# Up projection with half products from the second pair on, and residual loads in order of use

## The chip, the core and the metric

The kernel runs on one core of a Trainium2 chip. Its engines are TensorE (matmul; PE in the profile, with its weight loads as PEld), VectorE (DVE), ScalarE (ACT), GpSimd (POOL) and SyncE (SP), which issues most DMAs. The metric is the device time of one execution in microseconds.

## The reference

One layer of an encoder block on 512 tokens of width 1024, in float32: an input layernorm, a mixing part (a state-space scan beside an attention branch), a layernorm, a convolutional feed-forward network (FFN) of inner width 2816, and a last layernorm. The change lies in the FFN and at the two layernorms around it:

```python
def _conv_ffn(h, w_up, conv_w, conv_b, w_down):
    u = _causal_dwconv(h @ w_up, conv_w, conv_b)
    a, v = jnp.split(u, 2, axis=-1)
    return (jax.nn.silu(a) * v) @ w_down
...
        h = _layernorm(DN_ALPHA * h + mix.astype(h.dtype), ln1_g[l], ln1_b[l])
        f = _conv_ffn(h, ffn_w_up[l], ffn_conv_w[l], ffn_conv_b[l], ffn_w_down[l])
        h = _layernorm(DN_ALPHA * h + f.astype(h.dtype), ln2_g[l], ln2_b[l])
```

## The kernel before

**Arithmetic.** TensorE multiplies in a reduced form of float32 (fp32r). So that little is lost, each operand is split into a high part (ScalarE copies and rounds it) and a low part (VectorE takes the difference), and each product is three passes: high by high, low weight by high, high weight by low. A block of 128 output channels over all 1024 inputs and 512 tokens is 8 input tiles x 3 passes = 24 passes of 512 columns. A weight block is loaded by SP into one of four raw buffers (`wraw`), and split into one of three pairs `whi`, `wlo`.

**Up projection.** The 5632 outputs are 22 pairs: pair n holds 128 channels of the half `a` and the same 128 of the half `v`. `ORDER` lists the pairs in the order in which they are done. Pairs 0 to 3 are done as ordinary blocks. The first three blocks (pair 0 and half of pair 1) are done in two halves of the tokens, `slice(0, 256)` first, so that they can begin while the layernorm of the last token tiles still runs; the next five are whole. The 18 pairs in `SEVEN` go through `seven`: the pair of blocks is a 2x2 block matrix (two channel halves by two input halves of 512), the activation is one too (two input halves by two token halves, L_ and R_), and the product is made from seven half products rather than eight. Each half product is 4 input tiles x 3 passes = 12 passes of 256 columns.

Its seven half products need sums of blocks. The sums of the weights (`su_d` in DRAM) are formed ahead by DMA, in four steps a pair: a copy issued by SP (two transfers), and three adding DMAs issued by POOL (`add`), each of which waits for a split on VectorE (`last_lo`) so that they are spread. The list `ahead` holds these steps in order; `ahead_run(n)` runs the next n of them: every seventh step of the scan stage (`SUMS`, as long as more than 6 are left) and, for the last 6, in the up loop. The sums of the activation, T(0) to T(3) (`Thi`, `Tlo`), are formed by `form_T` from `h32`, a transposed copy of the layernorm's output: four sums or differences on VectorE, four high parts on ScalarE, four low parts on VectorE, each 128x1024. T(1) multiplies `y2`, T(2) `y3`, T(0) `y1` and T(3) `a22`; `a11`, `a12` and `y4` multiply plain activation. `chain[0]` makes TensorE's matmuls follow the program's order; elsewhere a list scheduler sets the order of an engine by priority and simulated time, with weight loads 400 places ahead (`high_priority`).

**Before it** stand the merge loop (`for n in range(KD)`, the attention branch's output blocks `w_br_att`), the output projection `w_out` and the layernorm. The layernorm goes by four token tiles of 128: statistics on VectorE, the root on POOL (`rs_y`), scaling on VectorE and POOL, transposes on TensorE into two PSUM buffers (`ptr`), and the eviction: high part and `h32` by ScalarE, low part (`h1lo`) by VectorE. The normalized tiles are also stored to `h1_d` as the residual for the end.

**After it** `up_out` adds the taps of the convolution (four operations on VectorE a pair) and the gate. The down projection is made of half products too; its VectorE and ScalarE operations are put in the order of written keys (`plan`, `at`), in microseconds from its start: `early` gives the keys of the weight blocks of its second part (17 of them, `w_next`), each split by `parts(k, k + 1.2, ...)`. The residual tiles are loaded again from `h1_d` during its first part, tiles 0 to 3 at c = 6 to 9; the additions (`res`) use tiles 2 and 3 first.

Of the kernel before, what the change touches and what calls it, by code (L numbers as in the profile page):

```python
# [16 lines left out]
P = 128  # L17
T = 512
# [56 lines left out]
def block_kernel(ctx, tc, A, out):  # L75
# [91 lines left out]
    last_pow, last_w, last_lo = [None], [None], [None]  # L167
# [9 lines left out]
    def split(hi, lo, src):  # L177
        nc.scalar.activation(hi, src, AF.Copy)  # L178
        return nc.vector.tensor_tensor(lo, src, hi.bitcast(F32), OP.subtract)  # L179
# [911 lines left out]
    ahead_run(len(ahead) - 6)  # L1091
# [78 lines left out]
    for n in range(KD):  # L1170
# [5 lines left out]
        proj(p, w, yT, part=(first, NP))  # L1176
        nc.vector.scalar_tensor_tensor(sg, sg, 1.0, p, OP.add, OP.mult)
# [26 lines left out]
    for k in range(KW, KD):  # L1204
        wo[k] = w_halves("w_out", k)
    l1r = {(n, j): wt("v", [P, T], "l1" + n) for j in range(2) for n in "gb"}
# [3 lines left out]
    for i in range(NT):  # L1210
# [8 lines left out]
        for j in range(2):  # L1219
# [12 lines left out]
            split(h1hi[:, ks, tok(i)], h1lo[:, ks, tok(i)], tr)  # L1232
            nc.scalar.activation(h32[j][:, :, tok(i)], tr, AF.Copy)
# [80 lines left out]

    def up_out(m, pa, pb):
# [6 lines left out]
        for j, p in enumerate((pa, pb)):  # L1322
# [3 lines left out]
            at(S, k(j, 0), nc.scalar.activation(y, p, AF.Identity, bias=fb[:, c:c + 1], scale=taps[2]))  # L1326
# [22 lines left out]
    def form_T():  # L1349

        b11, b12, b21, b22 = [t[:, :, c] for t in h32 for c in (L_, R_)]
        nc.vector.tensor_tensor(b11, b11, b12, OP.subtract)
        nc.vector.tensor_tensor(b12, b22, b12, OP.subtract)
        yield
        nc.vector.tensor_tensor(b22, b22, b11, OP.add)
        nc.vector.tensor_tensor(b21, b22, b21, OP.subtract)
        yield
        for j, t in ((1, b22), (2, b12), (0, b11), (3, b21)):
            if j == 1:
                nc.scalar.activation(Thi[:, j], t, AF.Copy, scale=-1.0)  # L1360
                nc.vector.scalar_tensor_tensor(Tlo[:, j], t, -1.0, Thi[:, j].bitcast(F32), OP.mult, OP.subtract)
            else:
                split(Thi[:, j], Tlo[:, j], t)
            if j == 2:
                yield
        yield
# [13 lines left out]
    def seven(m):  # L1380
# [18 lines left out]
        bank, W = tr_tile(), acc_tile()  # L1399
# [5 lines left out]
        product(W[:, R_], y3, Tq[2], first=True)  # L1405
        if m > 4:
            product(W[:, L_], a12, Bq[1, 0])
        product(U, y2, Tq[1])
        copy(2)
        if m == 4:  # L1410
            product(W[:, L_], a12, Bq[1, 0])
        yield
        y1, = w_block(S_[:, 1])
        product(U, y1, Tq[0])
# [31 lines left out]
    started = []  # L1446
    for s in range(3, 2 * KF + 1):
# [4 lines left out]
        if s < 8:  # L1452
            p = acc_tile() if s % 2 else any_tile("abc")
            proj(p, w_("w_up", 2 * ORDER[s // 2] + s % 2), h1T)
            pend.append(p)
        elif s == 2 * KF:
            pend += next(started.pop(0))
            chain[0] = False
        elif s % 2 == 0:
            if not started:  # L1460
                chain[0], last_pe[0] = True, None
            started.append(seven(s // 2))
# [4 lines left out]
        if s > 3:  # L1467
            with tc.issue_after(last_lo[0].ins):
                next(T_steps, None)
        if s == 36:  # L1470
            mark = last_w[0]
        if s >= 8 and s % 2 == 0:
# [3 lines left out]
        if s == 3:  # L1476
            for i in range(NT):
# [348 lines left out]
```

## Time and profile before

| | |
|---|---|
| median of 3 runs | 1072.49 us (1071.71 to 1072.97) |
| profiled execution, its own time | 1072.7 us |
| profiled execution, span of the trace | 1071.0 us |
| granted TensorE clock | 0.998 |
| DMA | 221.01 MB, mean 206 GB/s |

The page is read as follows. The busy line tells how long each engine ran; matmuls are pipelined, so a busy PE can still lose time by a slow pace, which is seen from the starts of its passes. The chain of waits follows the work that ended last back to the start, so pieces of one engine that follow each other without a gap are time that this engine alone sets. A row of a timeline gives start, length, engine, line, operation, output and inputs, and in brackets the idle time before it and what ended that. `L179` is a helper (`split`), so its operations are told apart by their tiles: `wlo` a weight block, `h1lo` the activation, `Tlo` a sum.

The stages that matter here, from the trace: merge loop and output projection from about 640 us, first pass of the up projection 728.5 us, first half product 775.4 us, down projection from 956.8 us, last matmul 1063.6 us, end 1071.0 us.

### The profile page before, as it was taken

The numbers are of one execution on the slowest core, as the hardware profiler recorded it, in microseconds if no ns is written. First come the engines' busy times: TensorE is split into PE (matmuls) and PEld (weight loads), VectorE is DVE, ScalarE is ACT, GpSimd is POOL, SyncE is SP. The second block draws the span as 40 slices with busy tenths as digits, with TensorE's granted clock in tenths as the row PEclk, the third lists the DMA queues.
The fourth block names the chain that finished last, engine by engine and source line by source line (L and its number), as shares of the span: only waits on it lengthen the run. The fifth ranks groups of instructions, "written<-read, shape, count | busy, mean of one in ns | idle before, by whom it ended". The sixth has DMA issues, their size and how long they took to land.

```text
span 1071.0 us, 16830 instructions
## 1 busy us (share of the span) xinstructions
PE 1058.5 (99%) x6045; PEld 910.4 (85%) x6045; DVE 879.3 (82%) x1583; ACT 557.2 (52%) x980; POOL 244.8 (23%) x282
## 2 busy tenths in 40 slices
PE   8999999999999999999999999999999999999997
PEld 7878888888888888888777878889899999998785
DVE  8667787886899997558998966756979989999797
ACT  6444664553635643345655533405566767765631
POOL 3010214313142334114454444042011000000001
PEclk9999999999999999999999999999999999999999
DMA  7878687999896885777998663744588766679763
GB/s 286 296 181 226 179 190 178 238 241 248 235 244 206 168 214 121 218 253 193 253 221 140 176 212 113 250 104 102 135 205 221 222 201 197 211 240 314 278 220 122
DMA packets 85794, 221.01 MB, mean 206 GB/s; under 512 B 9648, under 2 KB 14304, under 8 KB 85536
## 3 DMA queue, kind: packets, MB, share of 16 engines
q1 hardware_dynamic: 72064, 185.87, 53.3%
q0 software_dynamic: 13648, 34.09, 21.3%
q8 instruction: 47, 0.77, 0.3%
q14 instruction: 35, 0.29, 0.1%
HBM read 207.70 MB, written 76.18 MB: 265 GB/s over the span
## 4 chain that ended last, share of the span: by engine, by line
PE 90%; DVE 5%; DMA 3%; issue 1%; ACT 1%; SPq 0%; POOL 0%; DVEq 0%; ACTq 0%
PE pacc L254 53%; PE ptr L1391 10%; PE pacc L1391 7%; PE ptr L254 4%; PE pc L254 4%; PE pb L254 2%; PE pacc L278 2%; DMA wraw<-in_w_dq_dram 1%; PE pa L254 1%; PE ptr L278 1%; PE pa L257 1%; PE ptr L257 1%; PE pb L257 1%; DVE h1hi L1293 1%; DVE wlo L1293 1%
## 5 line engine op out<-in xcount | busy, mean ns | idle before, releaser
L254 PE MATMUL pacc<-hhi,whi 128*128 128x512 f32 (+1 forms) x536 | 216.3, 404 | 0.8 <-ACT hhi L429 0.8
L254 PE MATMUL pacc<-hlo,whi 128*128 128x512 f32 (+1 forms) x536 | 210.0, 392 | 0.5 <-DVE hlo L432 0.5
L254 PE MATMUL pacc<-hhi,wlo 128*128 128x512 f32 (+1 forms) x536 | 208.3, 390 | 0.1
L192 ACT ACTIVATE whi<-wraw 128x1024 fp32r<-128x1024 f32 x105 | 111.0, 1058 | 173.3 <-PE pacc L254 138.0
L193 DVE TENSOR_TENSOR wlo<-wraw,whi 128x1024 fp32r<-128x1024 f32 x105 | 137.9, 1313 | 56.7 <-ACT whi L192 56.5
L254 PEld LDWEIGHTS pacc<-hlo,whi 128*128 128x128 f32 (+1 forms) x536 | 100.4, 187 | 23.5 <-DVE hlo L432 1.8
L254 PEld LDWEIGHTS pacc<-hhi,whi 128*128 128x128 f32 (+1 forms) x536 | 100.8, 188 | 20.0 <-issue 1.4
L254 PEld LDWEIGHTS pacc<-hhi,wlo 128*128 128x128 f32 (+1 forms) x536 | 100.7, 188 | 18.2 <-DVE wlo L394 0.4
L178 ACT ACTIVATE whi<-wraw 128x1024 fp32r<-128x1024 f32 (+1 forms) x72 | 68.3, 949 | 54.4 <-PE ptr L1391 22.8
L179 DVE TENSOR_TENSOR wlo<-wraw,whi 128x1024 fp32r<-128x1024 f32 (+1 forms) x72 | 78.3, 1088 | 17.2 <-ACT whi L178 16.5
L1030 POOL TENSOR_TENSOR tm<-mask,toe 128x128 f32<-128x128 f32 (+1 forms) x64 | 44.5, 700 | 105.8 <-DVE mn L1047 92.7
L212 POOL DMA_DIRECT2D su_d<-su_d x36 | 30.7, 900 | 116.2 <-DVE wlo L193 51.9
L652 DVE SCALAR_TENSOR_TENSOR cv<-pacc,cwb,cv 128x511 f32<-128x511 f32 (+2 forms) x72 | 53.2, 740 | 0.3
L1050 ACT ACTIVATE l<-l,mn 128x128 f32<-128x128 f32 (+1 forms) x64 | 35.8, 560 | 31.8 <-DVE mn L1047 30.4
L254 PE MATMUL pacc<-yhi,whi 128*128 128x512 f32 x128 | 50.3, 394 | 0.0
L254 PE MATMUL pacc<-yhi,wlo 128*128 128x512 f32 x128 | 49.8, 389 | 0.0
L254 PE MATMUL pacc<-ylo,whi 128*128 128x512 f32 x128 | 49.8, 389 | 0.0
L1391 PE MATMUL ptr<-h1hi,wlo 128*128 128x256 f32 x144 | 40.8, 283 | 0.0
L1391 PE MATMUL ptr<-h1lo,whi 128*128 128x256 f32 x144 | 40.8, 283 | 0.0
L1391 PE MATMUL ptr<-Thi,whi 128*128 128x256 f32 x144 | 40.8, 283 | 0.0
L1391 PE MATMUL ptr<-Thi,wlo 128*128 128x256 f32 x144 | 40.8, 283 | 0.0
L1391 PE MATMUL ptr<-Tlo,whi 128*128 128x256 f32 x144 | 40.8, 283 | 0.0
(648 smaller groups left out, 2866.2 us busy)
## 6 DMA issues: line engine op xcount, KB each, us to landing
su_d<-in_w_up_dram SPq DMA_DIRECT2D x36, 512.0 KB, 8.1
wraw<-su_d SPq DMA_DIRECT2D x72, 256.0 KB, 4.0
wraw<-in_w_up_dram SPq DMA_DIRECT2D x54, 256.0 KB, 3.8
wraw<-in_w_xbc_dram SPq DMA_DIRECT2D x24, 512.0 KB, 6.2
su_d<-in_w_up_dram POOLq DMA_DIRECT2D x18, 512.0 KB, 10.9
su_d<-su_d POOLq DMA_DIRECT2D x36, 256.0 KB, 7.8
G<-ac_d SPq DMA_DIRECT2D x16, 512.0 KB, 6.1
wraw<-in_w_z_dram SPq DMA_DIRECT2D x16, 512.0 KB, 5.8
```

The lines of the kernel that those rows point to most:

```text
L178: nc.scalar.activation(hi, src, AF.Copy)
L179: return nc.vector.tensor_tensor(lo, src, hi.bitcast(F32), OP.subtract)
L192: nc.scalar.activation(hi[:, :cols], raw[:, :cols], AF.Copy)
L193: last_lo[0] = nc.vector.tensor_tensor(lo[:, :cols], raw[:, :cols], hi[:, :cols].bitcast(F32), OP.subtract)
L212: d = nc.gpsimd.dma_start(dst, src, accum_op=OP.add)
L254: pe(nc.tensor.matmul(p, a, b, start=start, stop=stop).ins)
L257: pe(nc.tensor.transpose(p, a, b).ins)
L278: nc.tensor.matmul(p, x[a][:, tok(i)], w[b][h], start=first and j == 0, stop=last and j == 2)
L652: nc.vector.scalar_tensor_tensor(y[:, d:], p[:, :T - d], cwb[:, 24 * k + c:24 * k + c + 1], y[:, d:], OP.mult, OP.add)
L1030: last_pow[0] = nc.gpsimd.tensor_tensor(tm[:, :K - f], maskt[i][:, f:], self.toe[:, 2 * P - K + f:], OP.add)
L1050: nc.scalar.activation(l[:, :K], l[:, :K], AF.Exp, bias=self.mn[:, ic], scale=-1.0, accum_out=self.sm[:, ic])
L1391: pe(nc.tensor.matmul(p, w[x_][:, tok(k)], r[k][y_], start=first and k + j == 0, stop=last and k == 3 and j == 2, skip_group_check=True).ins)
```

## The change

- Pairs 1, 2 and 3 join `SEVEN`: 21 of 22 pairs go through `seven`. Only pair 0 is ordinary; both its blocks are done in token halves L_ and R_. Between the two halves stands the first step of pair 1: the products of `a11` and `a12` with L_, which need no T.
- `form_T` no longer works on 256-column halves after the layernorm. `form_T(q)` forms the sums of token tiles q and q + 2, in operations of 128x512: q = 0 can start when tile 2 is evicted, q = 1 when tile 3 is. The order of these operations and of tile 3's eviction on VectorE and on ScalarE is written out by hand (`behind`), and so is what follows them: pair 0's first eviction behind the high part of T(0), pair 1's `y1` split behind T(1), T(3)'s low part behind pair 2's splits.
- In pair 1 the products come in another order (`a11`, `a12`, then `y2` with T(1), then `y3` with T(2)), and `a12`, `y2` are split into four single tiles of the pool `xs` (`w_apart`), since the three pairs `whi`, `wlo` are taken.
- The steps of the weight sums: 84 in all; the scan stage leaves 16 rather than 6; the merge loop runs one per block (8); the up loop one at every fourth half pair (8) rather than at every second from s = 8.
- The store of a normalized tile to `h1_d` is written directly behind its layernorm rather than after the up projection's first blocks.
- Down projection: residual tiles 2 and 3 are loaded at c = 7 and 8, tiles 0 and 1 between the first loads of the second part, each into the other one of the two buffer tags; the keys of weight blocks 15 and 16 go from 90 and 92.5 to 88.1 and 88.5.

```diff
-SEVEN = (4, 5, 16, 6, 7, 17, 8, 18, 9, 19, 10, 11, 20, 12, 13, 14, 15, 21)
-ORDER = (0, 1, 2, 3, *SEVEN)
+SEVEN = (1, 2, 3, 4, 5, 16, 6, 7, 17, 8, 18, 9, 19, 10, 11, 20, 12, 13, 14, 15, 21)
+ORDER = (0, *SEVEN)
-SUMS = (5, 7, 6)
+SUMS = (5, 7, 16)
...
-    ahead_run(len(ahead) - 6)
+    ahead_run(len(ahead) - 16)
...
         proj(p, w, yT, part=(first, NP))
+        ahead_run(1)
...
-            split(h1hi[:, ks, tok(i)], h1lo[:, ks, tok(i)], tr)
-            nc.scalar.activation(h32[j][:, :, tok(i)], tr, AF.Copy)
+            parts_of[i].append([nc.scalar.activation(h1hi[:, ks, tok(i)], tr, AF.Copy),
+                                nc.vector.tensor_tensor(h1lo[:, ks, tok(i)], tr, h1hi[:, ks, tok(i)].bitcast(F32),
+                                                        OP.subtract),
+                                nc.scalar.activation(h32[j][:, :, tok(i)], tr, AF.Copy)])
+        nc.sync.dma_start(h1_d[:, i], h1[i])
...
+    def behind(b, a):
+        tc.add_manual_dep(b.ins, a.ins.name, NOSYNC, reason="order")
...
+            if m == j == 0:
+                behind(a, h1_[0])
...
+    def form_T(q):
+
+        b11, b12, b21, b22 = [t[:, :, c] for t in h32 for c in (tok(q), tok(2 + q))]
+        hi, lo = [[t[:, j, :, tok(q)] for j in range(4)] for t in (Thi, Tlo)]
+        b = [nc.vector.tensor_tensor(b11, b11, b12, OP.subtract), nc.vector.tensor_tensor(b12, b22, b12, OP.subtract),
+             nc.vector.tensor_tensor(b22, b22, b11, OP.add)]
+        h, l = {}, {}
+        for j, t in ((2, b12), (1, b22), (0, b11), (3, b21)):
+            if j == 3:
+                b.append(nc.vector.tensor_tensor(b21, b22, b21, OP.subtract))
+            h[j] = nc.scalar.activation(hi[j], t, AF.Copy, scale=-1.0 if j == 1 else 1.0)
             if j == 1:
+                l[j] = nc.vector.scalar_tensor_tensor(lo[j], t, -1.0, hi[j].bitcast(F32), OP.mult, OP.subtract)
             else:
+                l[j] = nc.vector.tensor_tensor(lo[j], t, hi[j].bitcast(F32), OP.subtract)
+        return b, h, l
+
+    def w_apart(*srcs):
+
+        with tc.high_priority(offset=400):
+            raw = wrw.tile([P, D], F32, name="wraw", tag="wraw")
+            blocks = [[wt("xs", [P, T], "wx", F32R) for _ in range(2)] for _ in srcs]
+            for j, src in enumerate(srcs):
+                last_w[0] = nc.sync.dma_start(raw[:, half_of(j)], src)
+            for j, b in enumerate(blocks):
+                last_lo[0] = split(*b, raw[:, half_of(j)])
+        return blocks
...
-        a12, y2 = w_block(a[:, T:], S_[:, 2])
+        a12, y2 = (w_block if m > 1 else w_apart)(a[:, T:], S_[:, 2])
+        if m == 2:
+            behind(l0[3], last_lo[0])
...
+        if m == 1:
+            product(W[:, L_], a12, Bq[1, 0], first=True)
+            yield
+        if m > 1:
+            product(W[:, R_], y3, Tq[2], first=True)
             product(W[:, L_], a12, Bq[1, 0])
         product(U, y2, Tq[1])
         copy(2)
+        if m == 1:
+            product(W[:, R_], y3, Tq[2])
         yield
         y1, = w_block(S_[:, 1])
+        if m == 1:
+            behind(last_hi[0], h1_[1])
+            behind(last_lo[0], l1[1])
...
-    w = [w_("w_up", s) for s in range(3)]
-    accs = [acc_tile() for _ in range(3)]
-    for ts in (slice(0, 2 * P), slice(2 * P, T)):
-        for j in range(3):
+    w = [w_("w_up", s) for s in range(2)]
+    accs = [acc_tile() for _ in range(2)]
+    started = []
+    for ts in (L_, R_):
+        for j in range(2):
             proj(accs[j][:, ts], w[j], [[x[:, ts] for x in h] for h in h1T])
-    T_steps = form_T()
-    next(T_steps)
+        if not started:
+            chain[0], last_pe[0] = True, None
+            T0 = form_T(0)
+            started.append(seven(1))
+            next(started[0])
+    T1 = form_T(1)
+    (b0, h0, l0), (b1, h1_, l1), ((s0, v0, c0), (s1, v1, c1)) = T0, T1, parts_of[3]
+    for line_ in ([*b0[:3], l0[2], l0[1], v0, v1, *b1[:3], l1[2], l1[1], l0[0], l1[0], b0[3], b1[3], l0[3], l1[3]],
+                  [h0[2], h0[1], s0, s1, c0, c1, h0[0], h1_[2], h1_[1], h1_[0], h0[3], h1_[3]]):
+        for a, b in zip(line_, line_[1:]):
+            behind(b, a)
...
-        if s >= 8 and s % 2 == 0:
+        if s % 4 == 0:
             ahead_run(1)
...
-    early = {0: 48, 1: 51.3, 2: 53, 3: 56.2, 4: 62.5, 11: 82.2, 12: 83.8, 13: 85.6, 14: 87.5, 15: 90, 16: 92.5}
+    early = {0: 48, 1: 51.3, 2: 53, 3: 56.2, 4: 62.5, 11: 82.2, 12: 83.8, 13: 85.6, 14: 87.5, 15: 88.1, 16: 88.5}
...
+    def load_h1(i):
+        h1[i] = wt("k4" if i > 1 else "g4", [P, D], "h1")
+        with tc.issue_after(last_w[0].ins):
+            nc.sync.dma_start(h1[i], h1_d[:, i])
+
...
+        if 6 < c < 9:
+            load_h1(c - 5)
...
-            for _ in range(4):
+            for i in (None, 0, 1, None):
                 w_next()
+                if i is not None:
+                    load_h1(i)
```

More of the change, by code (lines that the diff above doesn't have):

```diff
@@ L177, in split @@
     def split(hi, lo, src):
-        nc.scalar.activation(hi, src, AF.Copy)
+        last_hi[0] = nc.scalar.activation(hi, src, AF.Copy)
         return nc.vector.tensor_tensor(lo, src, hi.bitcast(F32), OP.subtract)
@@ L1205, in block_kernel @@
         wo[k] = w_halves("w_out", k)
+    parts_of = [[] for _ in range(NT)]
     l1r = {(n, j): wt("v", [P, T], "l1" + n) for j in range(2) for n in "gb"}
@@ L1325, in up_out @@
             taps = [nfw[:, i, n:n + 1] if j and n in SEVEN else fw[:, 44 * i + c:44 * i + c + 1] for i in range(3)]
-            at(S, k(j, 0), nc.scalar.activation(y, p, AF.Identity, bias=fb[:, c:c + 1], scale=taps[2]))
+            a = at(S, k(j, 0), nc.scalar.activation(y, p, AF.Identity, bias=fb[:, c:c + 1], scale=taps[2]))
+            if m == j == 0:
+                behind(a, h1_[0])
             uv.append((y, p, taps))
@@ L1398, in seven @@
         q_ = [uv[:, j * TH:(j + 1) * TH] for j in range(4)]
-        bank, W = tr_tile(), acc_tile()
+        bank, W = tr_tile() if m > 1 else ps("a"), acc_tile()
         U = bank[:, L_]
         a11, y3 = w_block(a[:, :T], S_[:, 0])
-        a12, y2 = w_block(a[:, T:], S_[:, 2])
+        a12, y2 = (w_block if m > 1 else w_apart)(a[:, T:], S_[:, 2])
+        if m == 2:
+            behind(l0[3], last_lo[0])
         product(U, a11, Bq[0, 0], first=True)
         copy(0)
-        product(W[:, R_], y3, Tq[2], first=True)
-        if m > 4:
+        if m == 1:
[3 more added lines that the diff above has]
+            product(W[:, R_], y3, Tq[2], first=True)
             product(W[:, L_], a12, Bq[1, 0])
@@ L1435, in seven @@
         yield [uv[:, half_of(j)] for j in range(2)]
-    w = [w_("w_up", s) for s in range(3)]
-    accs = [acc_tile() for _ in range(3)]
-    for ts in (slice(0, 2 * P), slice(2 * P, T)):
-        for j in range(3):
-            proj(accs[j][:, ts], w[j], [[x[:, ts] for x in h] for h in h1T])
-    T_steps = form_T()
-    next(T_steps)
+    w = [w_("w_up", s) for s in range(2)]
[3 more added lines that the diff above has]
+        for j in range(2):
+            proj(accs[j][:, ts], w[j], [[x[:, ts] for x in h] for h in h1T])
+        if not started:
[9 more added lines that the diff above has]
+            behind(b, a)
     pend = accs
     done = 0
-    started = []
-    for s in range(3, 2 * KF + 1):
+    for s in range(2, 2 * KF + 1):
         if len(pend) >= 2 and done < KF - 2:
@@ L1459, in block_kernel @@
         elif s % 2 == 0:
-            if not started:
-                chain[0], last_pe[0] = True, None
-            started.append(seven(s // 2))
+            if s > 2:
+                started.append(seven(s // 2))
             next(started[-1])
@@ L1475, in block_kernel @@
             third.pop(0)()
-        if s == 3:
-            for i in range(NT):
-                nc.sync.dma_start(h1_d[:, i], h1[i])
     tp_c.__exit__(None, None, None)
```

35 lines of the change are left out of this document (3 added, 32 removed).

## Prediction

> **What bounds the kernel now.** I read the page first, then the busy time by stretches, then the waits of TensorE, and last the chain of waits.
>
> ```profile
> span 1071.0 us, 16830 instructions
> 728.40:775.40 47.00, 47.00 (x283) 41.88 (x283) 38.70 (x52) 27.02 (x36) 4.93 (x6) 1.00 0.43 108
> 740.10:775.40 35.30, 35.30 (x188) 30.41 (x187) 31.63 (x39) 21.03 (x26) 2.24 (x3) 1.00 0.42 111
> 775.40:956.80 181.40, 181.40 (x1513) 181.40 (x1513) 163.31 (x233) 127.03 (x211) 11.93 (x18) 1.00 0.74 214
> 956.80:1063.70 106.90, 106.08 (x474) 86.70 (x472) 95.49 (x138) 53.38 (x69) 4.05 (x5) 1.00 0.71 245
> ```
>
> The last four rows are stretches: length, then busy time of PE, PEld, DVE, ACT and POOL, granted clock, DMA share. From the first up-projection pass (728.5) to 956.8 TensorE is never idle, at clock 1.00, and in the down projection it lacks 0.8 us. So a matmul taken out is worth its pace, and any new wait of PE is a loss of the same size. VectorE is second: 163.31 of 181.40 us in the seven-product stretch, 9.07 per pair.
>
> The paces come from the chain of waits (start, length, what):
>
> ```profile
> 728.50 4.06 PE pacc L254 x30
> ...
> 737.62 0.44 PE ptr L1230 x4
> ...
> 747.97 5.65 PE pb L254 x24
> ...
> 769.93 5.44 PE pacc L254 x24
> 775.38 1.43 PE ptr L1391 x12
> ...
> 956.81 1.44 PE ptr L254 x6
> ```
>
> An ordinary 512-column block is 24 passes in 5.44 us, 0.2267 each, so an ordinary pair of blocks takes 10.88. The 18 seven-product pairs run from 775.38 to 956.81: 10.08 us a pair, 84 passes of 256 columns at 0.1200. A half pass costs more than half a full one (0.1133).
>
> **The change: TensorE.** Before, 728.50 to 775.38 (46.88 us) holds 144 half passes (three blocks, two token halves), 120 full passes (five blocks) and the last 16 transposes (four groups of 0.44, 1.76). By pace: 17.28 + 27.20 + 1.76 = 46.24; the other 0.64 is edges, 0.21 of it at the change of width (5.65 against 5.44). After, the same work is 96 half passes (pair 0) and three seven-product pairs, 252: 348 x 0.1200 + 1.76 = 43.52, with 0.43 of edges 43.95. **The term is 46.88 - 43.95 = -2.9 us.** It is 0.80 per converted pair plus 0.5 from the third block, which loses the half-width price.
>
> The page "TensorE: Matmul & The Clock Gate" of the Trainium skill, section "Back-to-back issue gap", gives N/2.4 + 2.5 ns for an isolated pass, 109 and 216 ns here; by that the same count would be -3.6 us (an estimate). It also says that weight load and matmul set the spacing together, and the trace agrees with that: PEld is busy 181.40 of 181.40 us where the passes are half as wide. The trace's 0.1200 and 0.2267 are what I use.
>
> **The entry: can the sums be ready?** Before, forming T was covered by five ordinary blocks. Now pair 1 needs T(1) right after the right-half passes of pair 0.
>
> ```profile
> 737.46 0.60 PE L1230 MATMUL ptr<-ident,h 128*128 128x128 f32 x4
> 738.73 1.36 DVE L179 TENSOR_TENSOR h1lo<-ptr,h1hi 128x512 fp32r<-128x512 f32 x2 [3.70 <-ACT h1hi L178]
> 740.09 1.23 DVE L1352 TENSOR_TENSOR h<-h 128x1024 f32<-128x1024 f32 x1
> 734.39 1.27 ACT L1233 ACTIVATE h<-ptr 128x512 f32<-128x512 f32 x2
> 738.10 1.27 ACT L178 ACTIVATE h1hi<-ptr 128x512 fp32r<-128x512 f32 x2 [2.44 <-PE ptr L1230]
> 739.45 1.27 ACT L1233 ACTIVATE h<-ptr 128x512 f32<-128x512 f32 x2
> 709.25 23.83 SPq L1478 DMA_DIRECT2D h_d<-h  x4
> ```
>
> A T operation on one token tile is 128x512, so 0.68 on VectorE (two in 1.36) and 0.64 on ScalarE (two in 1.27); there are 16 on VectorE where 8 wide ones of 1.23 stood. Tile 2's copies end at 735.66 and tile 3's transposes only start at 737.46, so the first five T operations on VectorE (3.4 us) and two on ScalarE fall mostly into the 3.70 us in which VectorE waits now. Then: ScalarE evicts tile 3 (four operations, 738.10 to 740.7); the second difference starts with the last copy, 740.7 to 741.4; the sum to 742.1, beside the high part of T(2); low part of T(2) to 742.8, beside the high part of T(1); low part of T(1) to 743.5. TensorE arrives later: now the half passes end at 747.97, and the left half stays at 72 passes (48 of pair 0, 24 of pair 1, which need no T), so the right half ends 24 passes sooner, at 747.97 - 2.88 = 745.1. **Margin 1.6 us.** T(0), wanted two products later at 748.0, needs two more low parts (1.4 us) and stands well.
>
> What queues behind these waits: on VectorE, behind the hand order, the low parts of the next weight blocks and pair 0's taps; on ScalarE, pair 0's first eviction, put behind T(0). TensorE waits for the blocks within 3 to 7 us. I allow 0.4 us for a late piece; the ends are 0 (the margin holds) and the 4.4 us of the VectorE rival below; 0.4 because the sum above ends early. In the layernorm, pair 1 adds two 128x512 splits, 1.4 us of VectorE in 690 to 728, and costs nothing while gaps like the 3.70 exist; without that cover it would move tile 3 by 1.4 us at most. The activation stores now stand ahead of the loads in the program, but SP's queue already spends 709 to 733 on them and the next blocks are loaded behind them, with no wait of PE: nothing.
>
> **The sums formed by DMA.** Three more pairs are 12 more steps (84 instead of 72): 2 more in the scan stage, 8 in the merge loop, 8 instead of 6 in the up loop.
>
> ```profile
> su_d<-in_w_up_dram SPq DMA_DIRECT2D x36, 512.0 KB, 8.1
> su_d<-su_d POOLq DMA_DIRECT2D x36, 256.0 KB, 7.8
> 703.81 1.01 POOL L174 TENSOR_TENSOR rs_y<-rs_v,mhalf 128x1 f32<-128x1 f32 x1 [48.57 <-DVE rs_v L172]
> 640.00:690.00 50.00, 50.00 (x227) 40.30 (x226) 33.10 (x40) 19.00 (x25) 11.47 (x8) 1.00 0.56 183
> ```
>
> In the merge loop POOL sits idle 48.57 us before the first root and DMA runs at 0.56, so six adds there wait for nobody who matters, and the 4 MB (some 12 us at the 346 GB/s of the fullest stretch below) fit in the 22 us left open. If they did not, the w_out blocks would come late; I hold a 0 with 0 to 1 us. A step in the up loop waits on POOL for a VectorE split; behind it stand only other DMAs. The last is issued at s = 32, five pairs before its use.
>
> **The down projection.** Two waits can go.
>
> ```profile
> 985.00:1001.00 16.00, 16.00 (x73) 13.23 (x72) 15.90 (x24) 12.37 (x20) 0.00 (x0) 1.00 0.97 346
> 1001.80 6.56 DMA wraw<-in_w_dq_dram
> 1011.14 0.61 PE L254 MATMUL ptr<-h1hi,fy 128*128 128x512 f32 x2
> 1011.95 1.20 PE L254 MATMUL ptr<-h1hi,fy 128*128 128x512 f32 x4 [0.20 <-DVE h1hi L1293]
> 1012.99 1.20 PE L254 MATMUL pc<-h1hi,fl 128*128 128x512 f32 x3
> 1014.03 0.86 PE L254 MATMUL pacc<-h1hi,fl 128*128 128x512 f32 x3
> 1051.71 1.28 DVE L1293 TENSOR_TENSOR h<-h,ptr 128x512 f32<-128x512 f32 x2
> 1052.90 1.34 DVE L1685 BATCH_NORM_STATS2 ln_sd<-h 128x6 f32<-128x512 f32 x3
> 1054.63 0.39 PE L254 MATMUL pacc<-h1lo,fl 128*128 128x512 f32 x1
> 1055.42 0.50 PE L254 MATMUL pacc<-h1lo,f 128*128 128x512 f32 x1 [0.41 <-DVE h1lo L1293]
> 1055.75 1.55 PE L254 MATMUL pacc<-h1lo,fl 128*128 128x512 f32 x6
> ```
>
> At 1055.42 the pass should start at 1054.86; with the next, 0.66 us is lost, because the low parts of weights 15 and 16 stand behind two additions and three statistics (2.6 us). Their keys move ahead of those; nothing on TensorE waits for the additions: **-0.65**. From 1011.14 to 1014.03 nine passes take 2.89 us, 0.85 more than their pace: a weight block needed 6.56 us to land after 16 us at DMA share 0.97. Two of the four residual loads leave that stretch (1 MB, about 3 us at 346 GB/s) and come behind the next weight loads. I take half, **-0.4**, between 0 and -0.85; the moved loads are wanted only by additions that follow the first half of this projection.
>
> **Sum:** -2.9 + 0.4 - 0.65 - 0.4 = -3.5. The profiled execution took 1072.7 us (its span and 1.7 around it), the median of the runs is 1072.49; from the median, **1069.0 us**.
>
> **Rivals.**
> *The entry stalls.* Every wide split (1.23) that gets in front of T(1) on VectorE delays it by as much; three or four of them, 3.7 to 4.9 us, less the margin of 1.6, are a wait of 2.1 to 3.3 in place of my 0.4. For it: five handoffs between ScalarE and VectorE in a row, each of which can meet such a split. Against: the order written by hand keeps T's operations together. From 1068.6 without a stall: 1070.7 to 1071.9.
> *VectorE becomes the bound, slower than before.*
>
> ```profile
> L179 DVE TENSOR_TENSOR wlo<-wraw,whi 128x512 fp32r<-128x512 f32 (+1 forms) x70 | 75.9, 1084 | 16.6 <-ACT whi L178 15.9
> L1434 DVE TENSOR_TENSOR uv<-uv,pacc 128x512 f32<-128x512 f32 x17 | 11.6, 683 | 1.7 <-PE pacc L1391 1.7
> L1420 DVE TENSOR_TENSOR uv<-uv,pacc 128x256 f32<-128x256 f32 x17 | 7.0, 414 | 0.0
> ```
>
> A seven-product pair costs VectorE 75.9/18 + 0.68 + 0.41 = 5.3 us of splits and additions, an ordinary one two wide splits, 2.5: 8.5 more for three pairs. From 740.1 to the same point VectorE then has 31.6 + 8.5 - 3.4 (T done earlier) = 36.7 us in 35.3 - 2.9 = 32.4: 4.4 over, with roundings. If none of it may lag and the two down edits give nothing, the time is 1072.5 - 2.9 + 4.4 = 1074.0. It decides from the point where the taps of pairs 1 and 2 have to stand ahead of weight splits. Against it: a seven-product pair's result lies in SBUF, so its taps may lag, and each pair leaves 10.08 - 9.07 = 1.0 us to catch up. The same skill page, section "The HAM clock gate", says that an idle window of about 3.4 us halves the clock; such a stall would then cost more, and no row here shows one.
> *The down edits do nothing,* since the load was late for another reason: 1072.5 - 2.9 + 0.4 = 1070.0.
> *The pairs do not get their sums in time:* the last sums come five pairs, 50 us, before use against 7.8 us to land; this would cost single waits, about 1071.
>
> **How the numbers follow.** Forecast 0.65 (1067.9 to 1070.3), entry stall 0.16, VectorE bound 0.08, down edits without effect 0.08, late sums 0.03. A measurement of this kernel tells about 0.2% (2.1 us) from no change. The forecast and half of the down-edit case are under 1070.35: faster 0.69. The entry stall, the other half, late sums and a part of the VectorE case are within: 0.24. Slower: 0.07. The range goes from 1067.8 (both waits gone, no stall, and a little) to 1071.8, most of the entry stall.
>
> **What would show it.** Pair 0 in 256-column passes, then 84 passes per pair at 0.1200, the seven-product stretch 211.7 us long with PE 100% busy; T's last low part for pair 1 before TensorE arrives; no wait of PE on h1lo near the end; first weight of the B half landing in about 4 us. The prediction is wrong if PE shows idle time of over 1 us between 738 and 775, or if VectorE is full there with ScalarE and PE waiting behind it.

## The result and the profile after

The changed kernel takes 1079.84 us in the median (1078.88 to 1081.6) against 1072.73 of the kernel before (1071.71 to 1073.72): ratio 1.0065, 95% interval 1.0053 to 1.0077. It is slower by 0.65%; I had forecast 1069.0 and a range up to 1071.8.

The page of the changed kernel, its first lines and its DMA queues (packets, MB, share of 16 engines):

```profile
span 1077.1 us, 17110 instructions
...
PE 1059.2 (98%) x6129; PEld 913.7 (85%) x6129; DVE 894.0 (83%) x1604; ACT 565.5 (52%) x1003; POOL 256.1 (24%) x291
...
q1 hardware_dynamic: 75472, 191.37, 55.2%
q0 software_dynamic: 14944, 37.23, 22.9%
...
wraw<-su_d SPq DMA_DIRECT2D x84, 256.0 KB, 4.3
```

The last row, from the DMA issues, is the loads of weight sums: count, size, and median us to landing.

TensorE's busy time hardly moved (1058.5 before), while the span grew by 6.1 us: the time went into waits and, in part, into a lower clock (last section). Where, is read from the same four marks in both traces: the first attention pass that opens the merge stage, the first up-projection pass, the first down-projection pass, and the end. Each mark is the start of the first such row in TensorE's timeline:

| us | merge starts | first up pass | first down pass | end | merge stage | up projection | down projection |
|---|---|---|---|---|---|---|---|
| before | 640.77 | 728.44 | 956.64 | 1071.0 | 87.67 | 228.20 | 114.36 |
| after | 640.34 | 734.58 | 962.62 | 1077.1 | 94.24 | 228.04 | 114.48 |
| expected | | | | | 87.7 | 225.7 | 113.3 |

So 6.6 us are lost in the merge stage (with the output projection and layernorm behind it), where the change moves DMAs, reorders the layernorm's evictions and adds two weight splits; the up projection gains 0.2 instead of 2.5 (2.9 less the 0.4 that I allowed for a late piece); the down projection gains nothing instead of 1.05. The busy times by stretches of the changed kernel (columns as in the prediction):

```profile
640.00:690.00 50.00, 46.42 (x207) 36.66 (x206) 32.65 (x33) 15.54 (x20) 17.55 (x12) 0.99 0.74 187
690.00:735.00 45.00, 44.59 (x198) 35.95 (x197) 30.07 (x50) 10.88 (x17) 16.25 (x15) 0.97 0.67 173
735.00:775.00 40.00, 40.00 (x334) 39.69 (x333) 36.10 (x54) 28.48 (x48) 5.14 (x6) 1.00 0.63 159
775.00:831.00 56.00, 54.70 (x448) 53.72 (x447) 50.65 (x77) 39.07 (x66) 5.74 (x8) 1.00 0.79 205
831.00:957.00 126.00, 126.00 (x1053) 126.00 (x1052) 116.31 (x167) 90.73 (x152) 7.90 (x12) 1.00 0.75 220
```

In 640 to 690 DMA's share rose from 0.56 to 0.74 while its rate stayed at 187 GB/s (183 before): the DMA engines are busier at almost the same rate. The entry, 735 to 775, is full, as forecast. From 831 on TensorE is full again; the up projection's loss lies in 775 to 831.

The chain of waits of the changed kernel, in the merge stage and in the first seven-product pairs:

```profile
668.23 10.88 DMA wraw<-in_w_out_dram
...
679.13 1.07 ACT wo L192
...
680.22 0.56 DVE wo L193
...
681.36 0.69 DVE mlo L1182
682.05 0.61 DVE sg L1178
...
690.47 9.62 DMA wraw<-in_w_up_dram
...
785.38 7.78 DMA wraw<-su_d
...
807.06 7.83 DMA wraw<-su_d
```

A w_out block is 10.88 us in flight. ScalarE and VectorE, in order, sit on its split (wo), and behind that stand the merge's own operations (mlo, then sg) and the next weight split (wlo), for which TensorE then waits. Its load starts at 668.23, between the adding DMAs that GpSimd issues there:

```profile
664.00 0.80 POOL L212 DMA_DIRECT2D su_d<-in_w_up_dram  x1
664.55 1.96 POOL L212 DMA_DIRECT2D su_d<-su_d  x2
671.92 0.82 POOL L212 DMA_DIRECT2D su_d<-in_w_up_dram  x1 [5.41 <-DVE wlo L193]
```

Later two loads of weight sums take 7.8 us each, against the median of 4.3; each starts within 2 us behind such an add (issued at 783.64 and 805.91). TensorE's waits in 636 to 736, 736 to 960 and 960 to 1080 (in total, times, longest):

```profile
PE pacc L278 <- DVE sg L1178: 1.8, 1, 1.8
PE ptr L278 <- DVE wlo L193: 1.7, 1, 1.7
PE ptr L278 <- DVE mlo L1182: 0.3, 1, 0.3
...
PE ptr L1410 <- DVE wlo L179: 0.6, 2, 0.3
PE ptr L1410 <- ACT uv L1414: 0.6, 1, 0.6
...
PE ptr L254 <- DVE h1lo L1298: 1.5, 1, 1.5
```

The waits of 0.4 and 0.2 us on h1lo and h1hi that ended the kernel before are gone, but a new one of 1.5 us on an earlier h1lo has come.

### The profile page after: what moved, and what is told of

The parts are those of the page before. It is cut to its first block, busy times and chain, and to the rows that moved or that the text cites. A ratio compares the mean times of both kernels' runs of the same rounds, so it can differ in the third digit from the quotient of the medians.

```text
span 1077.1 us, 17110 instructions
## 1 busy us (share of the span) xinstructions
PE 1059.2 (98%) x6129; PEld 913.7 (85%) x6129; DVE 894.0 (83%) x1604; ACT 565.5 (52%) x1003; POOL 256.1 (24%) x291
## 4 chain that ended last, share of the span: by engine, by line
PE 86%; DVE 7%; DMA 5%; issue 2%; ACT 1%; POOL 0%; SPq 0%; DVEq 0%; ACTq 0%
PE pacc L254 50%; PE ptr L1410 8%; PE pacc L1410 6%; PE ptr L254 6%; PE pc L254 4%; PE pb L254 2%; PE pa L254 2%; DMA wraw<-su_d 1%; DMA wraw<-in_w_out_dram 1%; PE pacc L278 1%; DVE wlo L193 1%; PE pa L257 1%; DMA wraw<-in_w_up_dram 1%; PE ptr L257 1%; DVE wlo L179 1%
## 5 line engine op out<-in xcount | busy, mean ns | idle before, releaser
L192 ACT ACTIVATE whi<-wraw 128x1024 fp32r<-128x1024 f32 x99 | 104.6, 1057 | 160.8 <-PE pacc L254 130.9
L193 DVE TENSOR_TENSOR wlo<-wraw,whi 128x1024 fp32r<-128x1024 f32 x99 | 134.9, 1363 | 53.5 <-ACT whi L192 53.4
L178 ACT ACTIVATE whi<-wraw 128x1024 fp32r<-128x1024 f32 x83 | 78.6, 947 | 54.0 <-PE ptr L1410 26.4
L179 DVE TENSOR_TENSOR wlo<-wraw,whi 128x1024 fp32r<-128x1024 f32 x83 | 89.9, 1086 | 16.7 <-ACT whi L178 16.0
L212 POOL DMA_DIRECT2D su_d<-su_d x42 | 36.2, 914 | 136.2 <-DVE wlo L179 54.9
L1410 PE MATMUL pacc<-Thi,whi 128*128 128x256 f32 x164 | 46.4, 283 | 0.0
L1410 PE MATMUL pacc<-Thi,wlo 128*128 128x256 f32 x164 | 46.4, 283 | 0.0
L1410 PE MATMUL pacc<-Tlo,whi 128*128 128x256 f32 x164 | 46.4, 283 | 0.0
L1410 PE MATMUL ptr<-Thi,wlo 128*128 128x256 f32 x160 | 45.5, 284 | 0.6 <-DVE wlo L179 0.6
L1410 PE MATMUL ptr<-Thi,whi 128*128 128x256 f32 x160 | 45.5, 284 | 0.7 <-ACT uv L1414 0.6
```

The source lines that it names most:

```text
L178: last_hi[0] = nc.scalar.activation(hi, src, AF.Copy)
L192: nc.scalar.activation(hi[:, :cols], raw[:, :cols], AF.Copy)
L193: last_lo[0] = nc.vector.tensor_tensor(lo[:, :cols], raw[:, :cols], hi[:, :cols].bitcast(F32), OP.subtract)
L212: d = nc.gpsimd.dma_start(dst, src, accum_op=OP.add)
L1410: pe(nc.tensor.matmul(p, w[x_][:, tok(k)], r[k][y_], start=first and k + j == 0, stop=last and k == 3 and j == 2, skip_group_check=True).ins)
```

## The experiments

My theory: the steps that form weight sums by DMA cost both losses, since the packets of an adding DMA occupy the 16 DMA engines much longer than its bytes tell, and loads that TensorE needs come late. Rivals: the new order in the layernorm and the early stores; a bound by VectorE; in the merge stage, the order of the queues rather than bandwidth. The marks of all runs, read as above (one profiled execution each), beside their times:

| run | median us | ratio to before, 95% | merge starts | merge stage | up | down |
|---|---|---|---|---|---|---|
| no adds in merge | 1074.03 | 1.0011 to 1.0029 | 641.22 | 87.67 | 228.90 | 116.51 |
| before + adds in merge | 1076.78 | 1.0029 to 1.0063 | 640.72 | 90.68 | 228.18 | 114.32 |
| all adds in scan | 1071.09 | 0.9980 to 0.9999 | 642.17 | 87.67 | 225.43 | 114.63 |
| late w_out splits | 1079.46 | 1.0053 to 1.0083 | 640.63 | 94.40 | 229.06 | 114.21 |
| merge before w_out | 1077.16 | 1.0028 to 1.0058 | 640.46 | 91.59 | 228.51 | 115.24 |
| early copies | 1081.97 | 1.0069 to 1.0103 | 644.47 | 92.73 | 228.47 | 114.73 |
| plain copies in merge | 1072.39 | 0.9998 to 1.0017 | 640.74 | 87.90 | 227.53 | 113.83 |
| late adds in up | 1071.45 | 0.9984 to 1.0003 | 641.50 | 87.67 | 225.45 | 114.58 |
| down edits undone | 1071.64 | 0.9981 to 1.0006 | 643.94 | 87.67 | 225.45 | 115.34 |
| early layernorm loads | 1070.05 | 0.9970 to 0.9988 | 642.09 | 87.67 | 225.45 | 113.49 |
| the same, down undone | 1069.93 | 0.9970 to 0.9988 | 642.06 | 87.67 | 225.44 | 112.83 |
| sixteen late adds | 1083.54 | 1.0091 to 1.0119 | 640.90 | 87.67 | 239.90 | 113.43 |

**No adds in the merge loop.**

```diff
-SUMS = (5, 7, 16)
+SUMS = (5, 7, 8)
...
-    ahead_run(len(ahead) - 16)
+    ahead_run(len(ahead) - 8)
...
         proj(p, w, yT, part=(first, NP))
-        ahead_run(1)
```

> The changed kernel, with its eight steps of forming weight sums by DMA taken out of the merge loop and put into the scan stage before it; the rest is as changed. My theory: the adds in the merge loop take the DMA engines from the w_out blocks, and the split of a late w_out block then stands in front of the merge's own operations on ScalarE and VectorE; this costs the 6.1 us by which the first up-projection pass came later (734.63 against 728.50). Then that pass goes back to 728.0 to 729.5 here and the time to about 1073.5 (1072.5 to 1075). Rival 1: the early stores of the activations, the extra splits or the new order in the layernorm are at fault; then the first pass stays near 734 and the time at 1079 to 1080. Rival 2: eight more steps in the scan stage cost as much there; then the eviction that starts the merge stage at 640.3 comes at 644 to 646 and the time stays near 1079.

The merge stage is back at 87.67 us, to the hundredth what it was before, with the new layernorm order, splits and stores all in place. These cost nothing; the DMA steps cost all 6.6 us.

**The kernel before, with such steps in its merge loop.**

```diff
-SUMS = (5, 7, 6)
+SUMS = (5, 7, 14)
...
-    ahead_run(len(ahead) - 6)
+    ahead_run(len(ahead) - 14)
...
         proj(p, w, yT, part=(first, NP))
+        ahead_run(1)
```

> The kernel before, with one thing changed: eight of the steps of forming weight sums by DMA are issued in the merge loop instead of the scan stage. No part of the up projection, the layernorm or the down projection is touched. My theory: this alone makes the first up-projection pass 5 to 7 us later and the time about 1078.5 (1076.5 to 1080). Rival: the steps find room beside the merge, as I predicted, and the time stays at 1072 to 1073.5.

They make it slower by themselves, without any other part of the change, but by 3.0 us in the merge stage and not 5 to 7. The sign of the theory stands, the size doesn't: something doubles the loss in the changed kernel.

**The order of the queues.** Two tries. The first gave the late splits a lower priority; the order of instructions in the merge stage came out the same on VectorE, ScalarE, GpSimd and SyncE, so it is in effect a second run of the changed kernel (1079.46 against 1079.84) and tells nothing of the order.

> The changed kernel; the loads of the w_out blocks and the adds in the merge loop stay as they are, but the splits of w_out blocks 2 to 4 are given a later place in the order of ScalarE and VectorE, behind the merge's own operations. Theory A (order in the queues): the merge loses its time since its evictions stand behind a split that waits for a late block; then the loss falls from 6.1 to under 2 us, the first up pass comes at 729 to 731 and the time is 1074 to 1076. Theory B (bandwidth alone): what is needed itself comes too late, and the time stays at 1078 to 1080.

The second forces the order:

```diff
-        nc.scalar.activation(m[0], sg, AF.Copy, scale=0.5)
-        nc.vector.scalar_tensor_tensor(m[1], sg, 0.5, m[0].bitcast(F32), OP.mult, OP.subtract)
+        mh = nc.scalar.activation(m[0], sg, AF.Copy, scale=0.5)
+        ml = nc.vector.scalar_tensor_tensor(m[1], sg, 0.5, m[0].bitcast(F32), OP.mult, OP.subtract)
+        if n == 5:
+            gate_ = mh, ml
...
         wo[k] = halves(w_("w_out", k, dst=d))
+        for b_, a_ in zip((last_hi[0], last_lo[0]), gate_):
+            tc.add_manual_dep(b_.ins, a_.ins.name, NOSYNC, reason="order")
```

> The changed kernel with its eight steps of sums in the merge loop, but the order of ScalarE and VectorE is forced: the splits of w_out blocks 2 to 4 come behind the high and low part of merge block 5, so that no merge operation up to that block stands behind a w_out load. Theory A (the split of a late block blocks the queue): the loss in the merge stage falls from 6.1 to under 3 us, the first up pass comes before 731.5 and the time is 1074 to 1077. Theory B (whatever is needed is late by itself: the blocks themselves, since the adds take the DMA engines): TensorE waits for the blocks instead, the first up pass stays at 733 to 735.5 and the time at 1078 to 1081.

Neither end: the merge stage loses 3.9 us. Its chain of waits, and TensorE's waits in 636 to 736:

```profile
671.05 12.47 DMA wraw<-in_w_out_dram
...
PE pacc L278 <- DVE sg L1178: 3.3, 2, 2.0
```

The merge's operations up to block 5 no longer stand behind the block, but the block is still 12.47 us in flight, and the last merge operations wait behind it. The listed waits fall only from 3.8 to 3.3 us; most of the 2.6 us that the forced order gives back is clock, which stays at 1.00 here, while the changed kernel loses 1.7 us to a lower one (last section). So the late block remains the source. What the order alone is worth, with no merge operation left behind the block, these runs don't show.

**Copies or adds?** Each sum needs a plain copy before its adds.

```diff
     ahead_run(len(ahead) - 16)
+    for i in (6, 2):
+        ahead.pop(i)()
...
-        ahead_run(1)
+        if n not in (2, 6):
+            ahead_run(1)
```

> The changed kernel; of the eight steps in the merge loop the two copies (512 KB twice in each) are issued at the end of the scan stage instead, the six adds stay in the merge loop. If the loss starts with the copies, which stand in SP's queue before the loads that GpSimd waits for (its tensor operations ran 6 us later than before and beside VectorE's), most of it goes: first up pass before 731, time 1074 to 1076. If it is the adds, which take the DMA engines while w_out is loaded: first up pass at 733 to 735, time 1078 to 1080.

With the copies away the merge stage still loses 5.1 us, and TensorE's listed waits are no shorter (4.2 us against 3.8): it is the adds. The clock stays at 1.00 here, which is about the 1.5 us of difference. (The time is above what I expected since this run reached the merge stage 4.1 us later; 2.4 of that is a wait in the scan stage that I did not follow up.)

**Adding or bytes?** The six adds of the merge loop write instead of adding, so this kernel leaves six additions out and its result is not the layer's:

```diff
-            d = nc.gpsimd.dma_start(dst, src, accum_op=OP.add)
+            d = nc.gpsimd.dma_start(dst, src) if plain[0] else nc.gpsimd.dma_start(dst, src, accum_op=OP.add)
...
+        plain[0] = True
         ahead_run(1)
+        plain[0] = False
```

> The changed kernel, where the six adds in the merge loop move the same bytes over the same queue but write them plainly instead of adding them to what is there (six of the weight sums are left out, so they hold one operand alone). Theory: what costs the merge stage is that an adding transfer takes the DMA engines 2.2 times as long per byte (software queue 34.09 MB for 21.3% of the span, the other queue 185.87 MB for 53.3%); then its loss against before (merge start to first up pass 94.2 against 87.7) falls from 6.6 to between 1.5 and 4 us and the time to 1075 to 1077.5. Rival: the number of bytes or the place in the queue is what matters, adding or not; the loss stays at 5.5 to 7 us and the time at 1078.5 to 1080.5.

The loss is gone (87.90), more than the theory asked for. GpSimd's layernorm operations begin nearly as late here as in the changed kernel (648.08, against 649.78 there and 643.78 before), so their delay is not the cause. The DMA queues in 640 to 695 (packets, MB, share of 16 engines), first of the changed kernel, then of this run:

```profile
q1 hardware_dynamic: 3210, 8.82, 52.1%
q0 software_dynamic: 741, 1.87, 23.9%
```

```profile
q1 hardware_dynamic: 3941, 10.62, 60.9%
q0 software_dynamic: 496, 1.70, 8.6%
```

0.239 of 55 us for 1.87 MB are 7.0 us of packet time on all 16 engines per MB; written plainly, 0.086 of 55 us for 1.70 MB are 2.8. Adding costs 2.5 times as much per byte on the same queue, and that, not the bytes, is the loss of the merge stage. The Trainium skill says, on its page "DMA: Bandwidth & Descriptors", section "Issuing engines are not separate DMA queues", that DMAs run on the same 16 engines and interleave, whichever engine issued them; the trace agrees: adds that GpSimd issues hold up loads that SP issues (10.88 us for a w_out block). For comparison, the issues of the kernel before in 640 to 695; in the changed kernel the median of these eight loads is 4.6, so it is single blocks that come late:

```profile
wraw<-in_w_out_dram SPq DMA_DIRECT2D x8, 512.0 KB, 3.8
```

**All adds in the scan stage.**

```diff
-SUMS = (5, 7, 16)
+SUMS = (5, 6, 0)
...
-    ahead_run(len(ahead) - 16)
+    ahead_run(len(ahead))
...
         proj(p, w, yT, part=(first, NP))
-        ahead_run(1)
```

The up loop then finds no step left.

> The changed kernel with all 84 steps of forming weight sums by DMA in the scan stage, none in the merge loop and none in the up loop. My theory for the 2.6 us lost between 770 and 830: an add on the software queue makes the load of a weight sum issued right behind it land in 7.8 instead of 4.3 us, and VectorE, at 9.1 of 10.08 us a pair, cannot make up for it; with no adds there the up projection (first pass to first down pass) takes 225.3 to 225.8 instead of 228.2, and the time is 1070 to 1071.5. Rival 1: VectorE is the bound in the first seven-product pairs with or without adds; then the up projection stays at 227.5 to 228.5 and the time at 1073 to 1074. Rival 2: sixteen more steps in the scan stage cost something there, which would show at the eviction that starts the merge stage (640.3).

The up projection takes 225.43 us, 2.77 less than before; without an add beside it, the conversion of three pairs gives what I had worked out (2.9). VectorE is no bound; two stretches of this run, then the same two of the changed kernel:

```profile
801.00:811.00 10.00, 10.00 (x85) 10.00 (x85) 9.38 (x14) 6.68 (x13) 0.00 (x0) 1.00 0.78 214
811.00:821.00 10.00, 10.00 (x86) 10.00 (x85) 9.93 (x17) 7.82 (x15) 0.55 (x1) 1.00 0.62 179
```

```profile
801.00:811.00 10.00, 9.68 (x80) 9.39 (x79) 10.00 (x14) 7.15 (x12) 1.43 (x2) 1.00 0.70 164
811.00:821.00 10.00, 9.40 (x78) 9.20 (x78) 7.61 (x14) 5.77 (x10) 0.00 (x0) 1.00 0.78 239
```

VectorE is as full here (9.38, 9.93) and TensorE never waits. In the changed kernel the two late loads leave VectorE short (7.54 of 10 us in 791 to 801, 7.61 in 811 to 821), and behind each it is near its limit (10.00 in 801 to 811, 9.80 in 821 to 831). The price is in the scan stage: the merge starts 1.4 us later than before.

**Adds late in the up loop,** beside the edit of the run without adds in the merge loop:

```diff
-        if s % 4 == 0:
+        if s >= 20 and s % 2 == 0:
             ahead_run(1)
```

> The changed kernel with 76 steps of sums in the scan stage, none in the merge loop, and the last eight in the up loop from its step 20 on (every second step) instead of steps 4 to 32. Theory: an add costs TensorE something only in the first seven-product pairs, where VectorE is full; later VectorE has room, so the up projection stays at 225.3 to 226 as without any adds there, the scan stage gives back some 0.9 us against the run with all adds in it (merge start 641.3 against 642.24), and the time is 1069.5 to 1070.7. Rival: an add in the up loop costs about 1.2 us each where it meets a load, whatever the step; then the up projection takes 227 to 230 and the time is over 1072.

The up projection stays at 225.45 with eight steps in it, so where an add falls decides, not that it falls there. The time did not improve on the run with all of them in the scan stage (1071.45 and 1071.09, with spreads of over 2 us): the merge starts at 641.50 here, but at 642.09 and 642.06 in two later runs with the same steps in the scan stage, so the 0.9 us that I expected from there are not shown.

**How near the edge that is.** Sixteen late steps, one in each step of the loop, none in the merge loop, and 68 in the scan stage, with the edit of the layernorm's loads that is told below:

```diff
-        if s % 4 == 0:
+        if s >= 20:
             ahead_run(1)
```

> As the run with early layernorm loads, but 16 steps of sums late in the up loop (one in each of its steps from 20 on) and 68 in the scan stage, as many there as in the changed kernel. Theory: the scan stage then costs what it costs in the changed kernel (merge start 640.3 to 640.9 instead of 641.5), and VectorE has room for the sixteen; the time is 0.5 to 1 us under the run with eight late steps, 1068.7 to 1069.8. Rival: at one step per 5 us the adds slow the weight loads as in the first pairs, and TensorE loses 1 to 4 us in the up projection; the time is 1070.5 to 1073.

The rival came out, and worse than it said: 239.90 us. The first wait of TensorE, and the clock around it (stretches, columns as before):

```profile
852.39 0.58 PE L1409 MATMUL ptr<-Thi,whi 128*128 128x256 f32 x1 [3.34 <-ACT uv L1413]
```

```profile
841.00:846.00 5.00, 5.00 (x44) 5.00 (x43) 5.00 (x9) 4.17 (x8) 0.59 (x1) 1.00 1.10 254
846.00:851.00 5.00, 3.05 (x26) 2.85 (x24) 2.38 (x4) 0.04 (x1) 1.42 (x2) 1.00 1.02 347
851.00:856.00 5.00, 3.61 (x17) 3.61 (x18) 2.96 (x3) 3.19 (x5) 0.00 (x0) 0.50 1.06 278
856.00:861.00 5.00, 5.00 (x37) 5.00 (x37) 3.84 (x6) 3.00 (x6) 0.00 (x0) 0.82 0.84 254
```

The DMA engines are full (1.02 to 1.10; a share over 1 says that packet times overlap, so us per MB is packet time and not time in which nothing else could move). A load is late, TensorE waits 3.34 us, and then its clock is at 0.50 and 0.82: that is another 3.4 us lost (5 x 0.50 + 5 x 0.18), so the wait is paid twice.

**The down projection.** Both edits taken back, with all adds in the scan stage:

```diff
-    early = {0: 48, 1: 51.3, 2: 53, 3: 56.2, 4: 62.5, 11: 82.2, 12: 83.8, 13: 85.6, 14: 87.5, 15: 88.1, 16: 88.5}
+    early = {0: 48, 1: 51.3, 2: 53, 3: 56.2, 4: 62.5, 11: 82.2, 12: 83.8, 13: 85.6, 14: 87.5, 15: 90, 16: 92.5}
...
-        if 6 < c < 9:
-            load_h1(c - 5)
+        if 5 < c < NC - 1:
+            load_h1(c - 6)
...
-            for i in (None, 0, 1, None):
+            for _ in range(4):
                 w_next()
-                if i is not None:
-                    load_h1(i)
```

> The run with all adds in the scan stage, with both edits of the down projection undone: weights 15 and 16 split as late as before, and the four residual loads where they were before. Theory: the two edits removed waits of 0.85 and 0.66 us, but TensorE then ran into a new wait of 1.6 us for the low part of a weight that stands behind the second layernorm's loads on VectorE, so they gave nothing; then from the first down pass to the end it takes 114.0 to 114.4 here against 114.5 with the edits, and the time is 1070.5 to 1071.2. Rival: the edits are worth the 1.05 us that I predicted and something else in the stage got slower; then it takes 115.2 to 115.8 and the time is 1071.8 to 1072.4.

Between the two: 115.34 us against 114.63 in its one profile (of an execution of 1074.1 us, above its median), but the times of the two runs don't differ by more than their spread. It also shows that the new wait isn't made by the edits, since 0.9 us of it stands here. What makes it, the timeline of VectorE and TensorE with all adds in the scan stage tells:

```profile
1037.92 0.75 DVE L1725 SCALAR_TENSOR_TENSOR h<-h,ln_mv,l2g 128x512 f32<-128x512 f32 x1 [1.37 <-DMA l2g<-in_ln_g_dram]
1038.59 0.74 DVE L1730 SCALAR_TENSOR_TENSOR h<-h,rs_y,l2b 128x512 f32<-128x512 f32 x1
1039.98 0.75 DVE L1730 SCALAR_TENSOR_TENSOR h<-h,rs_y,l2b 128x512 f32<-128x512 f32 x1 [0.65 <-DMA l2b<-in_ln_b_dram]
1040.65 1.22 DVE L1297 TENSOR_TENSOR h1lo<-wraw,h1lo 128x1024 fp32r<-128x1024 f32 x1
...
1041.92 1.43 PE L254 MATMUL ptr<-h1lo,f 128*128 128x512 f32 x5 [1.65 <-DVE h1lo L1297]
```

VectorE sits 1.37 and 0.65 us on the scale and shift of the last layernorm, and the low part that TensorE needs is next in its order. So I moved these loads ahead of some weight loads, in the kernel with eight late steps in the up loop:

```diff
     for c in range(NC):
+        if c == 8:
+            l2r = {(n, j): wt("v", [P, T], "l2" + n) for j in range(2) for n in "gb"}
+            with tc.issue_after(last_w[0].ins):
+                for (n, j), t in l2r.items():
+                    nc.sync.dma_start(t, bcast(A["ln2_" + n][half_of(j)], T))
         if c % 2 == 0:
             w_next()
...
-    l2r = {(n, j): wt("v", [P, T], "l2" + n) for j in range(2) for n in "gb"}
-    with tc.issue_after(last_w[0].ins):
-        for (n, j), t in l2r.items():
-            nc.sync.dma_start(t, bcast(A["ln2_" + n][half_of(j)], T))
```

> The run with 76 steps in the scan stage and eight late in the up loop, with one more edit: the four loads of the second layernorm's scale and shift are issued some weight loads earlier in the down projection. Theory: TensorE's wait of 1.5 us for the low part of a weight comes since VectorE, in order, sits on those loads (1.4 and 0.6 us) ahead of it; then the wait goes, from the first down pass to the end it takes 112.7 to 113.2 instead of 114.4, and the time is 1069.5 to 1070.5. Rival: the weight block itself lands too late (5.96 us in flight), as the chain of waits has it; then the wait stays at 1 to 2 us and the time at 1071 to 1072.

> As the run with early layernorm loads, with both edits of the down projection undone. It tells what these edits are worth when the layernorm's loads are out of the way. My prediction had 1.05 us (0.65 for the two weights, 0.4 for the residual loads): from the first down pass to the end 113.8 to 114.3 here, and the time 1.0 to 1.4 us over that run. Rival: they are worth nothing, and the two times are the same.

The wait is gone in both (TensorE has none listed from 640 to the last pass), and both are faster than the kernel before: 0.9979 (0.9970 to 0.9988). With the loads moved, the two edits of the change are worth nothing: 1070.05 with and 1069.93 without. Neither old wait comes back without them, though the two additions and three statistics still stand ahead of the low parts on VectorE (from 1048.47, the low parts from 1050.92). That the position of the loads makes the wait is shown; whether by VectorE sitting on them or by the weight load beside them (5.96 us in flight in the chain) these runs don't separate.

## Why the prediction was wrong

By stages, after less before: scan -0.43, merge +6.57, up -0.16, down +0.12, sum +6.1.

- **The sums formed by DMA: the step that failed.** I held "a 0 with 0 to 1 us", by 4 MB at 346 GB/s, 12 us in 22 free. First, the rate was that of plain loads. The page of before already had the price of adds, in its DMA queues:

```profile
q1 hardware_dynamic: 72064, 185.87, 53.3%
q0 software_dynamic: 13648, 34.09, 21.3%
```

  The software queue, which carries the adds, takes 6.7 us of packet time on all engines per MB (0.213 of 1071 us by 34.09 MB), the other queue 3.1; the 2 MB of adds and 2 MB of copies are 13.4 + 6.1 = 19.5 us by these prices, which barely fits. Second, room on average was the wrong test: one w_out block 10.88 us in flight was enough, since its split stands in two in-order queues ahead of the merge's operations. "Wait for nobody who matters" looked at who waits for the adds, and not at whom the adds delay. I knew that case ("the w_out blocks would come late") and gave it at most 1 us and no chance of its own. It cost 6.6 us and should have been the rival on the slow side.
- **Adds in the up loop: the same step.** "Behind it stand only other DMAs": those are the weight loads. 2.6 us, nearly the whole TensorE term, was given back at two loads of 7.8 us. The kernel before issues six such adds in the same stretch (777.17 to 827.90) and TensorE waits for none; VectorE is busy there 8.45 and 8.61 of 10 us in 791 to 811, and 10.00 in 801 to 811 after the change. So it seems to take both, a late load and a VectorE without room; no run separates the two.
- **TensorE term: right.** -2.9 forecast, -2.77 measured (228.20 to 225.43) where no add stands beside it.
- **The entry: right.** The last piece of T(1) and TensorE's first product with it, in the changed kernel's timeline and chain:

```profile
749.14 0.69 DVE L1371 SCALAR_TENSOR_TENSOR Tlo<-h,Thi 128x512 fp32r<-128x512 f32 x1
...
751.39 1.44 PE pa L1410 x12
```

  It ends at 749.83, 1.6 us ahead, the margin I had. The 0.4 allowed for a late piece was not needed.
- **Layernorm, early stores, split halves: 0, right** (merge stage 87.67 wherever no step of the up projection's sums runs in the merge loop). Adds as such do not cost it: the kernel before issues eight for the down projection's sums (`sd_d`) from 704.79 to 732.9, in the same stage, and loses nothing. Where an add falls decides.
- **VectorE as the bound: right to hold as unlikely.** At 9.4 to 9.9 of 10 it delays nobody while no load is late; it has little room to make up a late load, and there the rival met the step that failed.
- **The down projection: wrong.** Both old waits went, as I said, and TensorE then met a wait of 1.45 us that the layernorm's loads make. "Nothing on TensorE waits for the additions" is true and not enough: I did not ask what is late next. My reason for the first wait, the operations ahead of the low parts, was not enough either: with the layernorm's loads early they stand there and nobody waits.
- **The range** ended at 1071.8 since no case in it priced what the adds take from other loads; the one case above it, VectorE as the bound (1074.0), is not what happened.

## What to carry to other kernels

Price a DMA by the engine time that its packets take, from its own queue's share over its own bytes in the page, and not by the rate of other transfers; then ask which load beside it lands late and what stands behind that load's first user in an in-order queue. A stage in which DMA looks half free on average can still have no room for a transfer whose neighbour is needed within a few us. And before a stall is booked as gain, look for the next operation on the same engine that will be late: here a wait of 1.5 us took the place of two that went.

## What I had not expected of the hardware

- An adding DMA took 7.0 us of packet time on all engines per MB against 2.8 for a plain one on the same queue, in the same place.
- **TensorE's clock can fall to half after a short wait.** In the run without adds in the merge loop, TensorE waited 1.83 us in the down projection, and the stretches behind it are (length, PE busy, clock, DMA share, GB/s):

```profile
1045.00:1048.00 3.00, 3.00 (x10) 0.63 0.66 195
1048.00:1051.00 3.00, 3.00 (x12) 0.80 0.86 294
```

  That is 1.7 us lost (3 x 0.37 + 3 x 0.20), 3.4 us at half speed; its down projection took 116.51. In the merge stage of the changed kernel, two waits of 1.73 and 1.77 us end at 684.56 and 688.21, and the clock there is 0.88 and 0.77 (columns as in the first table of busy times):

```profile
685.00:690.00 5.00, 3.23 (x13) 2.25 (x12) 4.97 (x7) 3.25 (x5) 0.00 (x0) 0.88 0.76 234
690.00:695.00 5.00, 5.00 (x18) 3.77 (x16) 4.92 (x9) 2.82 (x5) 0.00 (x0) 0.77 0.96 277
```

  That is 1.75 us (5 x 0.12 + 5 x 0.23), about as much again. The length of a wait alone does not decide it. A wait of 1.65 us in the run with all adds in the scan stage cost no clock, one of 2.4 us in the merge stage of the run with early copies cost none either, and the kernel before with adds and the run with the forced order waited 2.4 and 3.3 us there in two pieces, at clock 1.00. The Trainium skill, "TensorE: Matmul & The Clock Gate", section "The HAM clock gate", has a free-running window of about 3.4 us and a halved clock after an idle one. The 3.4 us at half speed agree with that window's length; a wait of 1.83 us is shorter than the idle window that the rule asks for, and here the measurement decides. The clock explains 1.7 of the 3.6 us by which the same kind of steps cost more in the changed kernel (6.6) than in the kernel before (3.0). Another 1.3 us are longer waits (TensorE is idle 4.0 us in 640 to 735 against 2.7); the rest is open.
- The merge stage took 87.67 us to the hundredth in eight kernels of different code around it: with no late load in its path, TensorE alone sets the stage.
